# Forgetting attention in a two-layer trunk: one tile for a pair's transposed weights, and the values products at the pair's end

## The chip, the cores and the metric

The kernel runs on one core of one Trainium2 chip. The metric is the device time of one execution in microseconds (us). The kernel before was timed three times: median 1266.29 us, from 1264.41 to 1266.33. One more execution was profiled.

## What is computed

A decoder trunk of two layers on one sequence of 512 tokens with 1024 channels, in float32. Each layer mixes (two groups of heads, joined by an output projection), adds the residual, normalizes, and then runs a gated feed-forward. Only the mixer of layer 0 is touched here. Its two groups are HGRN2 (a gated linear recurrence, 4 heads of 128) and forgetting attention (8 heads of 64). The second one, cut to what matters:

```python
def forgetting_attention(q, k, v, f_logit, b_f):
    log_f = jax.nn.log_sigmoid(f_logit + b_f)
    c = jnp.cumsum(log_f, axis=1).transpose(0, 2, 1)
    for blk in range(S // Q_BLOCK):                 # 4 blocks of 128 queries
        q0, q1 = blk * Q_BLOCK, (blk + 1) * Q_BLOCK
        logits = einsum('bqhd,bkhd->bhqk', q[:, q0:q1], k[:, :q1]) * FOX_DIM ** -0.5
        logits = logits + c[:, :, q0:q1, None] - c[:, :, None, :q1]
        logits = where(kpos <= qpos, logits, -inf)
        p = softmax(logits, axis=-1)
        outs.append(einsum('bhqk,bkhd->bqhd', p, v[:, :q1]))
```

The last line is the values product of this text: query block i needs the i+1 key blocks up to its own, so a head has 1+2+3+4 = 10 blocks of 128 queries by 128 keys.

## The kernel before, in words

**Projections.** Every large product is done three times with operands split into a high and a low part (`mm3`, L245 to L249: high by high on L247, high by low on L248 or L249, and low by high on the other). A projection (`proj`) is 8 such triples of 512 columns into one PSUM bank, 24 products; `values` (L284) is four token blocks of 24 products. Weights come by DMA into `ws` (two buffers), ScalarE casts the high part `wh` (L236), VectorE makes the low part `wl` (L237); `wh` and `wl` have five buffers.

**Layer 0** (`layer0`) runs over four heads h. For each it writes down an HGRN2 head, then a pair of forgetting-attention heads; with h = 0 also the forget gates (`fox_gates`, L556 to L576) and the values of all pairs (`values(S_VB)`, names `pv` and then `v`), and with h = 3 the output projection (names `po` from `wh`, L326 for the residual). A scheduler reorders all of this for each engine ahead of the run, by dependences and by which buffers are free; the order on an engine is then fixed.

**An HGRN2 head.** `acc` (L476) takes the diagonal products `dg` (L475); then seven levels each make a tile `E` (VectorE L485, ScalarE exp L486, VectorE L487), small products `sc` (L493) and a masked copy into `acc` (L497). Beside these goes a state: `kd` (L504 to L506), its transposes `kt` (L510), the copy `kdt` (L512), products `st` (L516), the exp `eb` (L518) and the running state `stt` (L520, L523). Then `o` (L529, L531), its square `sq` on ScalarE (L534), the mean `ms` on TensorE (L536), ln and exp on ScalarE (L537, L538), two products on VectorE (L539, L540) and the split into `yh` and `yl` (L242, L243).

**The forget gates.** Products `pf` (L556), copied by ScalarE to the tile `f` (L559), folded by the product `pfb` (L563), whose result goes through ScalarE (L567 to L569) and VectorE (L570, L571, the scan L573), a cast to `c16h` (L575) and L576. The tiles `f` and `c16h` are drawn from the buffers named `pT`.

**A pair of attention heads** (`fox_pair`). The q and k projections are split per head into `qk` and `k` (VectorE L595, L600, L601; ScalarE L592, L594, L599). Then for each of four query blocks i: scores `s` (L627 to L629), row maximum (L632 or L638), exp and division on ScalarE (L640, L645; reciprocal L641), transposes of p into the PSUM tile `pt` (L647), one or two copies to the SBUF tile `pT` (L650, L652), the values products (L660; 2(i+1) of them, 128 columns wide, each with 64 rows of outputs), and at once the split of the block's 128 columns into `yh` (ScalarE L664) and `yl` (VectorE L665). For i = 0 and 1 both heads share one `pt`, one `pT` and one copy. `behind` keeps the first values product after the block's copies in the schedule.

**Buffers of layer 0** (2 KB per partition each): `E` 3, `pT` 2, and one each of `kd`, `kdt`, `eb`, `stt`, `sq`.

In layer 1 stick-breaking attention has the same shape of values products, already at a pair's end (L826).

Of the kernel before, what the change touches and what calls it, by code (L numbers as in the profile page):

```python
# [7 lines left out]
F32 = mybir.dt.float32  # L8
F32R = mybir.dt.float32r
# [3 lines left out]
ALU = mybir.AluOpType  # L13
AX = mybir.AxisListType

P = 128
T = 512
D = 1024
NTB = T // P
# [34 lines left out]
class Trunk:  # L54
# [373 lines left out]
    def hgrn_head(self, h, z=None, qp=None):  # L428
        nc = self.nc
# [4 lines left out]
        e = self.t2k("e", tag="E")  # L434
# [6 lines left out]
        bb = self.t2k("bb", [P, 2, T], tag="bb")  # L441
# [8 lines left out]
        kq = self.t2k("kq", [P, 2, T], tag="kq")  # L450
# [8 lines left out]
        G = self.t2k("G", tag="G")  # L459
# [8 lines left out]
        v = self.va  # L468

        hs = slice(h * P, (h + 1) * P)  # L470
        acc = self.t2k("acc", tag="acc")
# [6 lines left out]
        for li, w in enumerate(LEVELS):  # L478
            n = T // (2 * w)
            vw = lambda a: a.rearrange("p (n two w) -> p n two w", two=2, w=w)  # L480
            E = self.t2k("E", tag="E")
# [7 lines left out]
            for c in range(4):  # L489
                cc = slice(c * P, (c + 1) * P)  # L490
                rhs = E[:, cc].rearrange("p (n two w) -> p n two w", two=2, w=w)[:, :, 1, :]
                for u in (0, 64)[:1 if w == 64 else 2]:
                    nc.tensor.matmul(ps[u:u + 64, c * 64:(c + 1) * 64], E[:, c * P + u:c * P + u + 64], rhs,  # L493
                                     start=True, stop=True)
            m = slice(0, 64 if w == 64 else P)
# [2 lines left out]
                                      lv.rearrange("p c (n w) -> p c n w", w=w),  # L498
                                      ps[m, 0:256].rearrange("p (c n w) -> p c n w", c=4, w=w))

        kd = self.t2k("kd", tag="kd")
        b3 = b[:, 0:384].rearrange("p (c t) -> p c t", t=P)
        kd3 = kd[:, 0:384].rearrange("p (c t) -> p c t", t=P)
        nc.vector.tensor_tensor(kd3, b3[:, :, P - 1:P].to_broadcast([P, 3, P]), b3, ALU.subtract)  # L504
# [2 lines left out]
        pt = self.bank("ho", "kt")  # L507
        for c in range(3):
            cc = slice(c * P, (c + 1) * P)
            nc.tensor.transpose(pt[:, cc], kd[:, cc], self.ident)  # L510
        kdt = self.t2k("kdt", tag="kdt")
        nc.scalar.copy(kdt[:, 0:384], pt[:, 0:384])  # L512
        pst = self.bank("ho", "st")
        for c in range(3):
            cc = slice(c * P, (c + 1) * P)
            nc.tensor.matmul(pst[:, cc], kdt[:, cc], v[c][:, hs], start=True, stop=True)  # L516
        eb = self.t2k("eb", tag="eb")
        A(eb, b, AF.Exp)  # L518
        st = self.t2k("stt", tag="stt")
        nc.vector.tensor_copy(st[:, 0:P], pst[:, 0:P])  # L520
        for c in (1, 2):
            cc = slice(c * P, (c + 1) * P)
# [3 lines left out]
        po = self.bank("ho", "o")  # L526
# [3 lines left out]
            if c:  # L530
                nc.tensor.matmul(po[:, cc], st[:, (c - 1) * P:c * P], eb[:, cc], start=False, stop=True)  # L531

        sq = self.t2k("sq", tag="sq")
        A(sq, po, AF.Square)  # L534
        pm = self.bank("sc", "ms")
        nc.tensor.matmul(pm, self.cmean, sq, start=True, stop=True)  # L536
# [4 lines left out]
        yh, yl = self.act("yh"), self.act("yl")  # L541
# [4 lines left out]
    def fox_gates(self):  # L546
        nc = self.nc
        st = self.t2k("wfs", [P, NKB * 32], tag="p")
        nc.sync.dma_start(st, self.ins["wfb"])
        xs = self.xt.rearrange("p b (k t) -> p (b k) t", t=T)  # L550

        pf = self.bank("g", "pf4")
        for i in range(2):
            for g in range(4):
                kb = 4 * i + g
                nc.tensor.matmul(pf[32 * g:32 * g + 32, :], st[:, 32 * kb:32 * kb + 32], xs[:, kb, :], start=i == 0,  # L556
                                 stop=i == 1)
        f4 = self.t2k("f4", tag="pT")
        nc.scalar.copy(f4, pf)  # L559
        fold = self.odd.tile([P, 16], F32, name="fold")  # L560
        nc.vector.tensor_reduce(fold, self.ident.rearrange("p (g m) -> p m g", m=32)[:, 0:16, :], axis=AX.X, op=ALU.add)
        ps = self.bank("g", "pfb")
        nc.tensor.matmul(ps[0:16, :], fold, f4, start=True, stop=True)  # L563
        bf = self.par[0:16, C_BF:C_BF + 1]
        a = self.t2k("fa", tag="p")
        m = self.t2k("fm", tag="p")
        nc.scalar.activation(a[0:16], ps[0:16, :], AF.Abs, bias=bf)  # L567
        nc.scalar.activation(a[0:16], a[0:16], AF.Exp, scale=-1.0)
        nc.scalar.activation(a[0:16], a[0:16], AF.Ln, bias=self.one[0:16])  # L569
        nc.vector.tensor_scalar(m[0:16], ps[0:16, :], bf, 0.0, ALU.add, ALU.min)  # L570
        nc.vector.tensor_tensor(a[0:16], a[0:16], m[0:16], ALU.subtract)  # L571
        nc.gpsimd.memset(m[0:16], 1.0)
        nc.vector.tensor_tensor_scan(a[0:16], m[0:16], a[0:16], 0.0, ALU.mult, ALU.add)  # L573
        h16 = self.t2k("c16h", [16, T], F32R, tag="pT")
        nc.scalar.copy(h16, a[0:16])  # L575
        nc.vector.scalar_tensor_tensor(self.c16, h16.bitcast(F32), self.par[0:16, C_LOSEL:C_LOSEL + 1], a[0:16],  # L576
                                       ALU.mult, ALU.add)
# [26 lines left out]
    def fox_pair(self, hp, v):  # L604
        nc = self.nc
        A = nc.scalar.activation
        k2 = self.k2[hp % 2]
        for e in range(2):
            o, h = 64 - 64 * e, 2 * hp + e
            nc.gpsimd.dma_start(k2[e][o:o + 2].bitcast(F32), self.c16[2 * h:2 * h + 2].bitcast(F32))  # L610
        q, k = self.qk_pair(S_QB + hp, S_KB + hp, k2, self.q2)
        yh, yl = self.act("yh"), self.act("yl")
        po = self.bank("po", "po")
        for i in range(NTB):
            n = (i + 1) * P
            c = slice(i * P, n)

            both = 2 * n <= T
            ss = []
            for e in range(2):  # L620
                if e and both:
                    s = ss[0][0], n
                else:
                    s = self.bank("s", "s"), 0
                ss.append(s)
                ps = s[0][:, s[1]:s[1] + n]
                nc.tensor.matmul(ps, q[e][:, c], k[e][:, 0:n], start=True, stop=False)  # L627
                nc.tensor.matmul(ps, self.q2[e][:, c], k2[e][:, 0:n], start=False, stop=False)
                nc.tensor.matmul(ps[:, c], self.identb, self.foxmask, start=False, stop=True)  # L629
            nm, rs, ri = [self.small(x, [P, 2]) for x in ("nm", "rs", "ri")]  # L630
            if both:
                nc.vector.tensor_reduce(nm, ss[0][0][:, 0:2 * n].rearrange("p (e n) -> p e n", e=2), axis=AX.X,  # L632
                                        op=ALU.max, negate=True)
            ts, cps = [], []
            for e in range(2):
                ps = ss[e][0][:, ss[e][1]:ss[e][1] + n]
                if not both:
                    nc.vector.tensor_reduce(nm[:, e:e + 1], ps, axis=AX.X, op=ALU.max, negate=True)  # L638
                p = self.t2k("p", tag="p")
                A(p[:, 0:n], ps, AF.Exp, bias=nm[:, e:e + 1], accum_out=rs[:, e:e + 1])  # L640
                nc.vector.reciprocal(ri[:, e:e + 1], rs[:, e:e + 1])  # L641
                A(p[:, 0:n], p[:, 0:n], AF.Copy, scale=ri[:, e:e + 1])
                if not (both and e):
                    pt, pT = self.bank("pt", "pt"), self.t2k("pT", tag="pT")
                t0 = n if both and e else 0  # L645
                for j in range(i + 1):
                    nc.tensor.transpose(pt[:, t0 + j * P:t0 + (j + 1) * P], p[:, j * P:(j + 1) * P], self.ident)  # L647
                ts.append((pT, t0))
                if not both:
                    nc.vector.tensor_copy(pT[:, 0:n], pt[:, 0:n])  # L650
                elif e:
                    nc.vector.tensor_copy(pT[:, 0:2 * n], pt[:, 0:2 * n])  # L652
            cp = self.newest()

            for j in range(i + 1):
                for e in range(2):
                    h = 2 * hp + e
                    d = slice(64 * e, 64 * e + 64)
                    pT, t0 = ts[e]
                    nc.tensor.matmul(po[d, c], v[j][:, h * 64:h * 64 + 64], pT[:, t0 + j * P:t0 + (j + 1) * P],  # L660
                                     start=j == 0, stop=j == i)
                    if j == 0 and e == 0:
                        self.behind(self.newest(), cp)
            nc.scalar.copy(yh[:, c], po[:, c])  # L664
            nc.vector.tensor_tensor(yl[:, c], po[:, c], yh[:, c].bitcast(F32), ALU.subtract)  # L665
        return yh, yl

    def layer0(self):
# [183 lines left out]
@with_exitstack  # L852
def hybrid_trunk_kernel(ctx: ExitStack, tc: tile.TileContext, out, **ins):
    t = Trunk(tc, ctx, ins, out)
    t.setup()
    with t.phase("l0", v=8, p=2, pT=2, E=3, bb=1, kq=1, G=1, acc=1, kd=1, kdt=1, eb=1, stt=1, sq=1) as t.ph, \
            tc.tile_pool(name="odd", bufs=1) as t.odd:
        y = t.layer0()
    with t.phase("f0", s=3, wah=4, wal=4) as t.ph:
        wa = t.out_rows(y, S_WO0 + 4, 0, S_FFN0)  # L860
        wa = t.ffn(S_FFN0, wa, 1, S_XR)
        xr = t.proj_halves(wa)
    with t.phase("l1", v=4, qk=7, kz=2, z=6, l=4, sh=5, sl=5) as t.ph:
# [109 lines left out]
```

## Time and profile before

| | us |
|---|---|
| median of three runs | 1266.29 |
| the profiled execution | 1266.0 |
| its span on the core | 1264.2 |
| mean granted TensorE clock in it | 0.994 |

A line of a timeline or of the chain gives start, duration (us), engine, line and operation; "[1.05 <-DVE qk L600]" says that the engine stood idle 1.05 us before it and what it waited for. PE is TensorE (PEld its weight loads), DVE VectorE, ACT ScalarE. A number after x counts the instructions that are put together; an f32 product such as L660 counts as two instructions in the profile, so that the 20 values products of a pair are 40 there.

### The profile page before, as it was taken

The numbers are of one execution on the slowest core, as the hardware profiler recorded it, in microseconds if no ns is written. First come the engines' busy times: TensorE is split into PE (matmuls) and PEld (weight loads), VectorE is DVE, ScalarE is ACT, GpSimd is POOL, SyncE is SP. The second block draws the span as 40 slices with busy tenths as digits, with TensorE's granted clock in tenths as the row PEclk, the third lists the DMA queues.
The fourth block names the chain that finished last, engine by engine and source line by source line (L and its number), as shares of the span: only waits on it lengthen the run. The fifth ranks groups of instructions, "written<-read, shape, count | busy, mean of one in ns | idle before, by whom it ended". The sixth has DMA issues, their size and how long they took to land.

```text
span 1264.2 us, 15623 instructions
## 1 busy us (share of the span) xinstructions
PE 1244.6 (98%) x6311; PEld 1006.6 (80%) x6311; DVE 690.3 (55%) x1039; ACT 485.3 (38%) x748; POOL 28.9 (2%) x51
## 2 busy tenths in 40 slices
PE   9999999999999999999999999999999999999997
PEld 6787777779888888888889776777988888888885
DVE  7538788769334333334377596786733333433437
ACT  7446557442322222222233757673322222222120
POOL 2000000000000000000000000000000000000001
PEclk9999999999999999999999998999999999999999
DMA  6332111133232233332324221102423332333321
GB/s 237 117 112 63 61 51 51 51 117 103 98 99 90 96 99 100 100 94 91 99 91 143 67 86 48 48 20 84 151 67 100 100 98 87 99 101 100 100 67 67
DMA packets 34984, 115.46 MB, mean 91 GB/s; under 512 B 4176, under 2 KB 5200, under 8 KB 34912
## 3 DMA queue, kind: packets, MB, share of 16 engines
q1 hardware_dynamic: 33504, 112.77, 28.3%
q10 hardware_dynamic: 1152, 1.66, 0.4%
q8 instruction: 49, 0.80, 0.2%
q14 instruction: 23, 0.19, 0.0%
q0 software_dynamic: 256, 0.03, 0.0%
HBM read 112.32 MB, written 2.10 MB: 91 GB/s over the span
## 4 chain that ended last, share of the span: by engine, by line
PE 89%; DVE 6%; DMA 2%; ACT 2%; issue 1%; SPq 0%; DVEq 0%; ACTq 0%
PE pf L248 13%; PE pf L247 13%; PE pf L249 13%; PE po L249 8%; PE po L247 8%; PE po L248 8%; PE pj L247 5%; PE pj L248 5%; PE pj L249 4%; DMA ws<-in_wst 2%; PE sc L493 1%; PE po L660 1%; PE cu L815 1%; PE pv L248 1%; PE pv L247 1%; PE tr L317 1%
## 5 line engine op out<-in xcount | busy, mean ns | idle before, releaser
L236 ACT CAST wh<-ws 128x1024 fp32r<-128x1024 f32 x177 | 186.4, 1053 | 525.8 <-PE pf L248 190.5
L237 DVE TENSOR_TENSOR wl<-ws,wh 128x1024 fp32r<-128x1024 f32 x177 | 216.5, 1223 | 308.8 <-ACT wh L236 302.9
L247 PE MATMUL pf<-xh,wh 128*128 128x512 f32 x640 | 249.0, 389 | 0.0
L248 PE MATMUL pf<-xl,wh 128*128 128x512 f32 x640 | 249.0, 389 | 0.0
L249 PE MATMUL pf<-xh,wl 128*128 128x512 f32 x640 | 249.0, 389 | 0.0
L249 PEld LDWEIGHTS pf<-xh,wl 128*128 128x128 f32 x640 | 120.1, 188 | 25.1
L247 PEld LDWEIGHTS pf<-xh,wh 128*128 128x128 f32 x640 | 120.1, 188 | 24.9
L248 PEld LDWEIGHTS pf<-xl,wh 128*128 128x128 f32 x640 | 120.1, 188 | 24.7
L247 PE MATMUL po<-wh,hh 128*128 128x512 f32 x352 | 137.4, 390 | 0.0
L249 PE MATMUL po<-wh,hl 128*128 128x512 f32 x352 | 137.1, 390 | 0.1
L248 PE MATMUL po<-wl,hh 128*128 128x512 f32 x352 | 137.0, 389 | 0.0
L415 DVE TENSOR_TENSOR s<-s,pf 128x512 f32<-128x512 f32 x44 | 30.3, 688 | 141.8 <-PE pf L249 140.4
L247 PE MATMUL pj<-xh,wh 128*128 128x512 f32 x256 | 104.6, 410 | 1.7 <-DVE qk L595 1.1
L249 PE MATMUL pj<-xh,wl 128*128 128x512 f32 x256 | 105.4, 412 | 0.0
L248 PE MATMUL pj<-xl,wh 128*128 128x512 f32 x256 | 103.6, 405 | 0.0
L249 PEld LDWEIGHTS po<-wh,hl 128*128 128x128 f32 x352 | 66.0, 188 | 14.5 <-DVE hl L243 0.7
L247 PEld LDWEIGHTS po<-wh,hh 128*128 128x128 f32 x352 | 66.1, 188 | 14.3 <-DVE xt L328 0.6
L248 PEld LDWEIGHTS po<-wl,hh 128*128 128x128 f32 x352 | 66.1, 188 | 13.5
L247 PEld LDWEIGHTS pj<-xh,wh 128*128 128x128 f32 x256 | 48.4, 190 | 14.2 <-issue 4.6
L249 PEld LDWEIGHTS pj<-xh,wl 128*128 128x128 f32 x256 | 48.4, 189 | 10.6 <-issue 2.3
L248 PEld LDWEIGHTS pj<-xl,wh 128*128 128x128 f32 x256 | 48.4, 189 | 10.1 <-issue 1.4
L328 DVE TENSOR_TENSOR xt<-xt,po 128x512 f32<-128x512 f32 x64 | 43.4, 685 | 14.8 <-PE po L249 14.7
(242 smaller groups left out, 1818.7 us busy)
## 6 DMA issues: line engine op xcount, KB each, us to landing
ws<-in_wst SPq DMA_DIRECT2D x189, 512.0 KB, 3.5
gb<-in_lnp SPq DMA_DIRECT2D x8, 512.0 KB, 4.8
ws<-in_wst SPq DMA_DIRECT2D x12, 256.0 KB, 5.2
xt<-in_xT SPq DMA_DIRECT2D x8, 256.0 KB, 4.9
xt<-in_x SPq DMA_DIRECT2D x1, 2048.0 KB, 7.8
out_y<-xt SPq DMA_DIRECT2D x4, 256.0 KB, 2.0
out_y<-xt ACTq DMA_DIRECT2D x4, 256.0 KB, 2.0
gw<-in_gw ACTq DMA_DIRECT2D x2, 256.0 KB, 3.2
```

The lines of the kernel that those rows point to most:

```text
L236: nc.scalar.copy(hi, st)
L237: nc.vector.tensor_tensor(lo, st, hi.bitcast(F32), ALU.subtract)
L247: mm(ps, ah, bh, start=first, stop=False)
L248: mm(ps, ah, bl, start=False, stop=False)
L249: mm(ps, al, bh, start=False, stop=last)
L317: nc.tensor.transpose(ps[:, j * P:(j + 1) * P], y[:, h * T + j * P:h * T + (j + 1) * P], self.ident)
L328: self.nc.vector.tensor_tensor(y, y, ps, ALU.add)
L415: nc.vector.tensor_tensor(s, s, pb, ALU.mult)
L493: nc.tensor.matmul(ps[u:u + 64, c * 64:(c + 1) * 64], E[:, c * P + u:c * P + u + 64], rhs, start=True, stop=True)
L660: nc.tensor.matmul(po[d, c], v[j][:, h * 64:h * 64 + 64], pT[:, t0 + j * P:t0 + (j + 1) * P], start=j == 0, stop=j == i)
L815: nc.tensor.matmul(ps[:, c:c + m], w, x[:, oi:oi + m], start=n == 0 and x is sh, stop=n == len(mms) - 1 and x is sl)
```

## The change

The transposed weights of a pair are kept in one tile `pT` of 20 blocks of 128 columns (10 KB, one buffer). Each head's transposes get a copy of their own (now L657), which writes to every fifth or sixth block, so that all queries that use one key block lie side by side: for head 0 in blocks 15, 10 and so on downwards with the transposes in reversed order, for head 1 upwards. After the fourth query block come eight values products, for key blocks j = 0 to 3 and two heads, of 512, 384, 256 and 128 columns (L664). The result is split once, 512 columns wide, by `put` (L242, L243). For i = 0 and 1 there are two copies to SBUF instead of one.

To make room, `kd`, `kdt`, `eb`, `stt` and `sq` lose their own buffers and are drawn from `E`, which has five buffers instead of three; `f` and `c16h` of the forget gates, that were drawn from `pT`, are drawn from `E` too.

```diff
-        kd = self.t2k("kd", tag="kd")
+        kd = self.t2k("kd", tag="E")
...
-        sq = self.t2k("sq", tag="sq")
+        sq = self.t2k("sq", tag="E")
...
-        f4 = self.t2k("f4", tag="pT")
+        f4 = self.t2k("f4", tag="E")
...
-        h16 = self.t2k("c16h", [16, T], F32R, tag="pT")
+        h16 = self.t2k("c16h", [16, T], F32R, tag="E")
...
+        pT = self.t2k("pT", [P, 20 * P], tag="pT")
+        at = ((15, -6), (1, 5))
...
-                if not both:
-                    nc.vector.tensor_copy(pT[:, 0:n], pt[:, 0:n])
-                elif e:
-                    nc.vector.tensor_copy(pT[:, 0:2 * n], pt[:, 0:2 * n])
+                    m = j if step > 0 else i - j
+                    nc.tensor.transpose(pt[:, t0 + m * P:t0 + (m + 1) * P], p[:, j * P:(j + 1) * P], self.ident)
+                lo = o + i + (0 if step > 0 else i * step)
+                dst = bass.AP(tensor=pT.tensor, offset=pT.offset + lo * P,
+                              ap=[pT.ap[0], [abs(step) * P, i + 1], [1, P]])
+                nc.vector.tensor_copy(dst, pt[:, t0:t0 + n].rearrange("p (j t) -> p j t", t=P))
+        cp = self.newest()
+
+        for j in range(NTB):
+            for e in range(2):
+                h = 2 * hp + e
+                x = (at[e][0] + at[e][1] * j + j) * P
+                nc.tensor.matmul(po[64 * e:64 * e + 64, j * P:T], v[j][:, h * 64:h * 64 + 64], pT[:, x:x + T - j * P],
+                                 start=j == 0, stop=j == NTB - 1)
...
-            nc.scalar.copy(yh[:, c], po[:, c])
-            nc.vector.tensor_tensor(yl[:, c], po[:, c], yh[:, c].bitcast(F32), ALU.subtract)
+        self.put(po, yh, yl)
...
-    with t.phase("l0", v=8, p=2, pT=2, E=3, bb=1, kq=1, G=1, acc=1, kd=1, kdt=1, eb=1, stt=1, sq=1) as t.ph, \
+    with t.phase("l0", v=8, p=2, pT=1, E=5, bb=1, kq=1, G=1, acc=1) as t.ph, \
```

The change moves more than its own lines. TensorE's order in head 0, before: `sc` are the level products, `pfb` the folding of the gates, `pv` the first token block of the values projection.

```order
L493 MATMUL sc_514<-E_510 64x64 x8
L563 MATMUL pfb_622<-f_80_618,fold 16x512
L247 MATMUL pv_664<-wh_642,xh 128x512
L493 MATMUL sc_528<-E_524 64x64 x8
L248 MATMUL pv_664<-wl_643,xh 128x512
L249 MATMUL pv_664<-wh_642,xl 128x512
L247 MATMUL pv_664<-wh_642,xh 128x512
L248 MATMUL pv_664<-wl_643,xh 128x512
L249 MATMUL pv_664<-wh_642,xl 128x512
L493 MATMUL sc_542<-E_538 64x64 x8
```

The same place of the changed kernel (`kt` and `st` belong to the state, `o` and `ms` to the head's end):

```order
L493 MATMUL sc_528<-E_524 64x64 x8
L510 MATMUL kt_570<-ident,kd_566 128x128 x3
L516 MATMUL st_576<-v_305,kdt_574 128x128
L516 MATMUL st_576<-v_306,kdt_574 128x128
L516 MATMUL st_576<-v_307,kdt_574 128x128
L493 MATMUL sc_542<-E_538 64x64 x8
L493 MATMUL sc_556<-E_552 64x64 x8
L529 MATMUL o_587<-acc_465,v_305 128x128
...
L536 MATMUL ms_597<-sq_595,cmean 128x512
L563 MATMUL pfb_622<-f_80_618,fold 16x512
L247 MATMUL pv_664<-wh_642,xh 128x512
```

The folding and the whole first values block now stand behind the last level and behind `ms`, and the state's transposes and products stand between the levels. On ScalarE the copy of `f`, which the folding needs, has moved behind the square; before:

```order
L486 ACTIVATE E_524<-E_524 128x512
L559 COPY f_80_618<-pf_79_609 128x512
L486 ACTIVATE E_538<-E_538 128x512
L567 ACTIVATE fa_624<-pfb_622,par 16x512
L486 ACTIVATE E_552<-E_552 128x512
```

And in the changed kernel, where the copy takes a buffer of `E`, which are drawn in the order of the program, after `sq`:

```order
L518 ACTIVATE eb_580<-bb_252 128x512
L534 ACTIVATE sq_595<-o_587 128x512
L559 COPY f_80_618<-pf_79_609 128x512
L537 ACTIVATE sq_595<-ms_597,eps 128x512
L538 ACTIVATE sq_595<-sq_595 128x512
```

VectorE's order at the entry of the last pair (h = 3), before: `sq` and `yl` end the HGRN2 head, `wl` is a weight, `qk` and `k` are the two heads' keys, for which the scores wait.

```order
L539 TENSOR_TENSOR sq_2209<-sq_2209,o_2201 128x512
L540 TENSOR_TENSOR sq_2209<-sq_2209,G_2073 128x512
L237 TENSOR_TENSOR wl_2591<-ws_2588,wh_2590 128x1024
L243 TENSOR_TENSOR yl_2218<-sq_2209,yh_2217 128x512
L600 CAST qk_2223<-pj_2267 64x512
L601 TENSOR_TENSOR k_233<-pj_2267,qk_2223 64x512
L326 SCALAR_TENSOR_TENSOR xt<-xt,po_2459 128x512
L600 CAST qk_2223<-pj_2267 64x512
```

In the changed kernel:

```order
L539 TENSOR_TENSOR sq_2146<-sq_2146,o_2138 128x512
L600 CAST qk_2160<-pj_2204 64x512
L540 TENSOR_TENSOR sq_2146<-sq_2146,G_2010 128x512
L601 TENSOR_TENSOR k_233<-pj_2204,qk_2160 64x512
L237 TENSOR_TENSOR wl_2507<-ws_2504,wh_2506 128x1024
L243 TENSOR_TENSOR yl_2155<-sq_2146,yh_2154 128x512
L600 CAST qk_2160<-pj_2204 64x512
```

The first head's key moved ahead of the weight, the second head's stands behind the weight and `yl`. On TensorE, 9 instead of 12 products of the output projection lie ahead of this pair's first scores, 3 between them and the second part of those scores, and none between the first head's scores and the second's (4 before).

More of the change, by code (lines that the diff above doesn't have):

```diff
@@ L510, in hgrn_head @@
             nc.tensor.transpose(pt[:, cc], kd[:, cc], self.ident)
-        kdt = self.t2k("kdt", tag="kdt")
+        kdt = self.t2k("kdt", tag="E")
         nc.scalar.copy(kdt[:, 0:384], pt[:, 0:384])
@@ L516, in hgrn_head @@
             nc.tensor.matmul(pst[:, cc], kdt[:, cc], v[c][:, hs], start=True, stop=True)
-        eb = self.t2k("eb", tag="eb")
+        eb = self.t2k("eb", tag="E")
         A(eb, b, AF.Exp)
-        st = self.t2k("stt", tag="stt")
+        st = self.t2k("stt", tag="E")
         nc.vector.tensor_copy(st[:, 0:P], pst[:, 0:P])
@@ L633, in fox_pair @@
                                         op=ALU.max, negate=True)
-            ts, cps = [], []
             for e in range(2):
@@ L643, in fox_pair @@
                 if not (both and e):
-                    pt, pT = self.bank("pt", "pt"), self.t2k("pT", tag="pT")
+                    pt = self.bank("pt", "pt")
                 t0 = n if both and e else 0
+                o, step = at[e]
                 for j in range(i + 1):
-                    nc.tensor.transpose(pt[:, t0 + j * P:t0 + (j + 1) * P], p[:, j * P:(j + 1) * P], self.ident)
-                ts.append((pT, t0))
-                if not both:
-                    nc.vector.tensor_copy(pT[:, 0:n], pt[:, 0:n])
-                elif e:
-                    nc.vector.tensor_copy(pT[:, 0:2 * n], pt[:, 0:2 * n])
[L653 to L665, printed above, removed]
+                    m = j if step > 0 else i - j
[11 more added lines that the diff above has]
+                                 start=j == 0, stop=j == NTB - 1)
+                if j == 0 and e == 0:
+                    self.behind(self.newest(), cp)
+        self.put(po, yh, yl)
         return yh, yl
```

## The prediction

> **What bounds the kernel now.** I read the page first, then the busy time by stage, then the chain, then timelines at the places that the change touches. The page gives the span and TensorE's share, and the chain of work that ended last gives its parts by engine.
>
> ```profile
> span 1264.2 us, 15623 instructions
> PE 1244.6 (98%) x6311; PEld 1006.6 (80%) x6311; DVE 690.3 (55%) x1039; ACT 485.3 (38%) x748; POOL 28.9 (2%) x51
> PE 89%; DVE 6%; DMA 2%; ACT 2%; issue 1%; SPq 0%; DVEq 0%; ACTq 0%
> ```
>
> TensorE is the bound: 98% busy and 89% of the chain. So two things count, TensorE's own work and the moments at which it has nothing to do. Layer 0 by stages shows the few of these; the columns are stretch, length, busy time of PE, PEld, DVE, ACT and POOL with their instructions, then the granted clock. The first stretch is the levels of head 0 to the end of the first values block, the next ones are the rest up to the end of pair 0, 1, 2 and 3.
>
> ```profile
> 46.15:66.00 19.85, 19.65 (x182) 12.75 (x180) 15.44 (x27) 9.60 (x16) 1.72 (x3) 1.00 0.48 173
> 66.00:121.00 55.00, 55.00 (x279) 42.49 (x278) 31.65 (x55) 30.41 (x60) 2.12 (x5) 1.00 0.27 81
> 169.70:218.50 48.80, 48.80 (x343) 36.32 (x343) 38.88 (x75) 29.72 (x62) 0.00 (x0) 1.00 0.14 45
> 218.50:266.00 47.50, 46.25 (x324) 33.87 (x323) 34.36 (x64) 24.47 (x51) 0.00 (x0) 0.96 0.22 74
> ```
>
> TensorE has no idle time in pairs 0 and 2 and 1.25 us in pair 3. What is taken from its work there shortens the run one for one, and a new gap lengthens it one for one.
>
> **Term 1, the values products: a gain of 6.3.** The chain shows all values groups of pair 2 (start, us, instructions), and the last row is layer 1's L826, which has the new form: 512, 384, 256 and 128 columns for two heads, in one group.
>
> ```profile
> 202.39 0.37 PE po L660 x4
> 206.25 0.59 PE po L660 x8
> 209.44 0.36 PE po L660 x2
> 210.47 0.80 PE po L660 x10
> 214.88 0.36 PE po L660 x2
> 215.90 1.02 PE po L660 x14
> 805.47 2.83 PE po L826 x14
> ```
>
> The six groups are 40 instructions and 0.37 + 0.59 + 0.36 + 0.80 + 0.36 + 1.02 = 3.50 us; the twin takes 2.83. Around a group something is lost as well, as TensorE's timeline shows in pair 0:
>
> ```profile
> 110.41 0.50 PE L248 MATMUL pj<-xl,wh 128*128 128x512 f32 x1
> 110.74 0.40 PE L249 MATMUL pj<-xh,wl 128*128 128x512 f32 x1
> 111.07 0.87 PE L660 MATMUL po<-pT,v 128*64 128x128 f32 x10
> 111.87 0.50 PE L247 MATMUL pj<-xh,wh 128*128 128x512 f32 x1
> 112.20 0.40 PE L248 MATMUL pj<-xl,wh 128*128 128x512 f32 x1
> 65.93 0.23 PE pv L249
> ```
>
> Projection products of 512 columns follow each other every 0.23 us (the last row, of the chain), but from 110.74 to the group's start are 0.33, and from the group's end (111.87) to the second product after it 0.33 again: 0.10 on entry and 0.10 on exit. Of the six groups five lie between projection products and are charged 0.20; the group of eight lies between score products, where I charge half. Before: 3.50 + 5 x 0.20 + 0.10 = 4.60. After: 2.83 + 0.20 = 3.03. The gain is 1.57 a pair, 6.3 for four. It is bounded by 4 x 0.67 = 2.7 (no entry or exit is real) and 4 x 1.67 = 6.7 (all six charged). I take 6.3, since the 0.33 stand right at such a group.
>
> The Trainium skill, page "TensorE: Matmul & The Clock Gate", section "Back-to-back issue gap", gives N/2.4 + about 2.5 ns from one product to the next; by an estimate from that, 40 instructions of 128 columns and 16 of 512 to 128 cost 2.23 and 2.17 us a pair, so that this term would be 0.2 and not 6.3. The rows speak against it: 1.02 us for 14 instructions of 128 columns is 73 ns each, not 56.
>
> **Term 2, head 0: a loss of 5.4.** Between the levels of head 0 TensorE waits for VectorE. Before, the folding `pfb` and the first values block filled these gaps. In the changed kernel both stand behind the last level, `o` and `ms`, since `f` needs a buffer of `E` and its copy stands behind the square on ScalarE. VectorE's waits between the levels, then the head's end in the chain and on the two other engines:
>
> ```profile
> 49.38 0.44 DVE L497 COPY_PREDICATED acc<-lvl,sc 64x256 f32<-64x256 uint8 x1 [1.22 <-PE sc L493]
> 50.87 0.46 DVE L497 COPY_PREDICATED acc<-lvl,sc 128x256 f32<-128x256 uint8 x1 [0.28 <-PE sc L493]
> 52.38 0.69 DVE L487 TENSOR_TENSOR E<-E,kq 128x512 f32<-128x512 f32 x1 [0.48 <-ACT E L486]
> 60.48 0.73 DVE L497 COPY_PREDICATED acc<-lvl,sc 128x256 f32<-128x256 uint8 x1 [0.75 <-PE sc L493]
> 61.39 0.61 PE L529 MATMUL o<-acc,v 128*128 128x128 f32 x4
> 62.87 0.48 PE L248 MATMUL pv<-wl,xh 128*128 128x512 f32 x1
> 63.27 0.58 ACT L534 ACTIVATE sq<-o 128x512 f32<-128x512 f32 x1
> 64.38 0.86 PE ms L536 x2
> 54.25 0.96 PE pfb L563 x2
> ```
>
> The last level's copy ends at 60.48 + 0.73 = 61.2. I leave it there: two weight casts (`wl`), the state's `kd` and `eb` come in among VectorE's level work, and four passes over `E`, `fm` and `fa` go out, about 3.8 us each way. Then, with nothing between: `o` from 61.4 to 62.9, the square from 63.27 to 63.85, `ms` 0.86 to about 64.9 with its start, `pfb` 0.96 to 65.9, and 24 products of 0.23, at 5.5 us, to 71.4. Before, this block was done at 66.0: plus 5.4. From there TensorE is busy for 55.00 of 55.00 us, so nothing takes the loss back. Lower bound: without any of the four waits (1.22 + 0.28 + 0.48 + 0.75 = 2.7) the copy ends at 58.5, and the loss is 2.7. Upper: the state's chain (exp, transposes, copy, products), that now stands between the levels, lies wholly on the path, at about 2.5 by its parts before: 7.9. I take the middle one, since both effects work on the same copies.
>
> **Term 3, the clock: a loss of 1.7.** In pair 3 TensorE stood idle once for over a microsecond, and the clock fell; the columns are those of the stages.
>
> ```profile
> 245.00:246.00 1.00, 1.00 (x4) 0.75 (x4) 0.97 (x2) 0.00 (x0) 0.00 (x0) 0.61 0.04 16
> 246.00:247.00 1.00, 1.00 (x5) 0.91 (x4) 0.17 (x1) 0.00 (x0) 0.00 (x0) 0.50 0.00 0
> 247.00:248.00 1.00, 1.00 (x6) 0.70 (x6) 0.40 (x1) 0.00 (x0) 0.00 (x0) 0.50 0.00 0
> 248.00:249.00 1.00, 1.00 (x5) 0.82 (x5) 0.47 (x3) 0.94 (x5) 0.00 (x0) 0.68 0.00 0
> 243.54 0.47 PE L627 MATMUL s<-qk 128*128 128x128 f32 x2 [1.05 <-DVE qk L600]
> ```
>
> The clock is lost for 0.39 + 0.50 + 0.50 + 0.32 = 1.7 of 4 us. Head 0 of the changed kernel has gaps of that size between its levels, one after another, and I charge one such fall there, 1.7, with bounds of none and of two and a half (4.0). The Trainium skill's same page, section "HAM oscillation — how this bites in real kernels", says "no PE-idle gaps >~3.4µs"; by that rule gaps of this size would cost no clock, and the sum below would be +1.6. This case's trace differs: a wait of 1.05 us was followed by the fall.
>
> **Term 4, the entries of the pairs: a loss of 1.5.** At a pair's entry TensorE's scores wait for the keys that VectorE splits. These rows are VectorE's in pair 3:
>
> ```profile
> 239.54 0.69 DVE L539 TENSOR_TENSOR sq<-sq,o 128x512 f32<-128x512 f32 x1 [3.57 <-PE pj L248]
> 240.88 1.22 DVE L237 TENSOR_TENSOR wl<-ws,wh 128x1024 fp32r<-128x1024 f32 x1
> 242.71 0.68 DVE L600 CAST qk<-pj 64x512 fp32r<-64x512 f32 x1
> ```
>
> In the changed kernel's order and with these durations, VectorE does `sq` at 239.54, the first L600 till 240.95, L540, the first L601 till 242.2, the weight till 243.3, `yl` till 244.0, the second L600 till 244.8 and L601 till 245.4. TensorE goes through the rest of the projection and 9 products till 241.1, the first scores till 241.5, 3 products and the second part of the scores till 242.8, and then waits for the second L600: 2.0, and 0.3 more for L601. That is 2.3 in place of 1.25, plus 1.0 (bounds: no wait at all, minus 1.3, and every split late by a weight's 1.22, plus 2.3). In pair 1 the same count ends within half a microsecond of a wait: 0.5 (0 to 2.5). In pair 2 none.
>
> **Term 5, the transposes: a loss of 1.0.** For i = 0 and 1 the second head's transposes write to the PSUM bank from which the first head's copy is now read, and wait for it. The nearest row is the 128-column split, the first one here:
>
> ```profile
> L665 DVE TENSOR_TENSOR yl<-po,yh 128x128 fp32r<-128x128 f32 x16 | 4.6, 287 | 2.4 <-ACT yh L664 2.2
> L664 ACT CAST yh<-po 128x128 fp32r<-128x128 f32 x16 | 4.2, 263 | 6.2 <-PE po L660 6.1
> ```
>
> Eight such copies of 0.29 are 2.3 if TensorE waits out each, and 0 if the projection's products cover them; with the copy itself queued on VectorE I take 1.0 (0 to 2.5).
>
> **Nothing** comes from the splits. Per pair ScalarE loses 4 x 0.263 and VectorE 4 x 0.287 and each gets one of 512 columns back; they are 38% and 55% busy, and after the pair's end the output projection is far off, except in pair 3, where later products cover it; uncovered it would cost one split, 0.6.
>
> **Sum:** -6.3 + 5.4 + 1.7 + 1.5 + 1.0 = +3.3. The profiled execution took 1266.0 (span 1264.2 and 1.8 around it), so 1269.3; it lies 0.3 under the median of the runs shown, so I say 1269.6 on their scale.
>
> **The rivals.** 0.2%, or 2.5 us, is about what a measurement of this kernel tells from no change.
>
> *A. Faster: VectorE doesn't wait.* Without the fillers TensorE serves each level at once, VectorE runs through head 0 without its 2.7 us of waits, and the state's chain hides beside it. With the clock whole and the entries free this gives -6.3 + 2.7 = -3.6: 1262.7. It decides once the last L497 of head 0 ends before about 59.6 and none of the other terms is there. For it: three of the four waits are for TensorE. Against: the state's chain now stands between the levels, and 3.8 us of new VectorE work. Chance 0.27.
>
> *B. No change to be measured.* Head 0 costs its 5.4, but gaps, entries and transposes together no more than 1.0: -6.3 + 5.4 + 1.0 = +0.1, so 1266.4. For it: most waits before were covered by projection products. Chance 0.24.
>
> *C. The half clock comes back.* A fall in pairs 1 and 3 and a second one in head 0 add 3 x 1.7 = 5.1: +8.4, 1274.7. The trace shows that one wait of 1.05 us is enough. Chance 0.10.
>
> *D. Products cost by their columns.* If a narrow product costs only its columns and entry and exit are hidden, 40 instructions at 73 ns are 2.92 against 2.83, and term 1 is 4 x 0.09 = 0.4 only: +9.2, 1275.5. Against it stand the 0.33. The Trainium skill's rule for the gap between products, weighed above, is of this kind. Chance 0.06.
>
> **How the numbers follow.** The forecast (slower by 0.26%, from 1268.8 to about 1272) has 0.33, so slower has 0.33 + 0.10 + 0.06 = 0.49, same 0.24, faster 0.27. The range goes from 1262.0, which holds most of A (its far end, 1261.4, has the entry of pair 3 free as well), to 1276.0, which holds C and D.
>
> **What would show it.** In head 0 of the changed profile: level products with idle time in front of them and no `pv` between, the last L497 at about 61, `pfb` after `ms`, the first `pv` block done at about 71, a granted clock below 1.00 near it. Values groups of L664 of about 2.83 with 0.33 at each end. An idle time of some 2 us before the second L631 in pair 3. The forecast is wrong if the first `pv` block is done by 69, if the clock stays whole through head 0, or if the values groups of a pair take over 4 us.

## The result, and the profile after

| | us |
|---|---|
| kernel before, median of 4 runs | 1266.19 (1264.41 to 1266.33) |
| changed kernel, median of 4 runs | 1274.65 (1272.92 to 1276.18) |
| ratio, 95% interval | 1.0069 (1.0053 to 1.0085) |
| profiled execution of the changed kernel | 1272.92, span 1270.8, mean granted clock 0.990 |

Slower, and by more than forecast: 8.5 us on the medians where 3.3 were said. The profiled execution is the fastest of the four; the other three took 1274.2 to 1276.2 us at a granted clock of 0.987. Of the changed kernel the page's span, busy times and chain by engine:

```profile
span 1270.8 us, 15388 instructions
PE 1243.4 (98%) x6215; PEld 1006.7 (79%) x6215; DVE 691.7 (54%) x1035; ACT 484.0 (38%) x736; POOL 28.8 (2%) x51
PE 87%; DVE 6%; ACT 3%; DMA 2%; issue 1%; SPq 0%; DVEq 0%; ACTq 0%
```

TensorE has 96 instructions and 1.2 us less to do, and the span is 6.6 us longer. So look for idle time. TensorE's timeline in head 0, its first products (`dg`) and then from the fourth level to the end of the first values block (some rows between are left out):

```profile
47.02 1.05 PE L475 MATMUL dg<-kq 128*128 128x128 f32 x8
54.79 0.69 PE L493 MATMUL sc<-E 128*64 128x64 f32 x16 [1.86 <-DVE acc L497]
56.70 0.69 PE L493 MATMUL sc<-E 128*64 128x64 f32 x16 [1.23 <-DVE acc L497]
62.24 1.12 PE L493 MATMUL sc<-E 128*64 128x64 f32 x16 [0.82 <-DVE acc L497]
64.19 1.22 PE L529 MATMUL o<-acc,v 128*128 128x128 f32 x4 [0.82 <-DVE acc L497]
68.30 1.12 PE L536 MATMUL ms<-sq,cmean 128*128 128x512 f32 x2 [0.75 <-ACT sq L534]
69.35 1.03 PE L563 MATMUL pfb<-f,fold 128*16 128x512 f32 x2
70.31 0.50 PE L247 MATMUL pv<-wh,xh 128*128 128x512 f32 x1
75.66 0.39 PE L249 MATMUL pv<-wh,xl 128*128 128x512 f32 x1
75.89 0.39 PE L247 MATMUL pv<-wh,xh 128*128 128x512 f32 x1
```

The levels now wait for VectorE's copies with no folding and no values product in between (the state's transposes and products stand between the fifth and the sixth), then come `o`, `ms`, `pfb`, and the first block's 24 products run from 70.31 to 75.89; before, they were done at 66.00. The level at 62.24 has 16 instructions like those at 54.79 and 56.70, but takes 1.12 us instead of 0.69: the clock. The folding is so late because ScalarE copies `f` only behind the square (before, at 53.53):

```profile
68.14 0.58 ACT L559 COPY f<-pf 128x512 f32<-128x512 f32 x1
```

The head also began a little later. In the profile of the kernel before, its first products stand here:

```profile
46.38 1.05 PE L475 MATMUL dg<-kq 128*128 128x128 f32 x8
```

The same stretch of the changed kernel by windows (before the last three columns, the granted clock):

```profile
46.38:57.00 10.62, 7.53 (x94) 4.30 (x94) 7.34 (x13) 4.25 (x6) 0.00 (x0) 1.00 0.67 213
57.00:68.00 11.00, 8.28 (x69) 6.91 (x65) 4.34 (x9) 1.36 (x3) 0.00 (x0) 0.53 0.44 178
68.00:75.89 7.89, 7.59 (x29) 5.02 (x29) 4.48 (x6) 5.05 (x9) 0.52 (x1) 1.00 0.01 2
```

For 11 us the clock was 0.53, though TensorE was busy for 8.28 of them; in the four us ahead of the fall (53 to 57) it had been busy for 0.98 only. The values groups of the four pairs, in the chain:

```profile
125.14 2.45 PE po L664 x15
172.29 2.76 PE po L664 x13
218.33 2.90 PE po L664 x14
267.06 2.92 PE po L664 x14
```

The entry of pair 3 in the changed kernel's timeline,

```profile
251.43 0.50 PE L631 MATMUL s<-qk 128*128 128x128 f32 x2 [1.82 <-DVE qk L600]
252.16 0.48 PE L632 MATMUL s<-k,q 128*128 128x128 f32 x1 [0.23 <-DVE k L601]
```

and the clock right after it, by windows:

```profile
252.00:256.00 4.00, 3.84 (x12) 3.15 (x13) 2.02 (x6) 1.50 (x6) 0.00 (x0) 0.57 0.25 102
```

That is 4 x 0.43 = 1.7 us of clock lost, as much as the fall in pair 3 of the kernel before. The end of layer 0, where the first transposes of the normalized rows start, before:

```profile
285.32 1.33 PE L317 MATMUL tr<-ident,xt 128*128 128x128 f32 x8
```

and in the changed kernel:

```profile
291.16 1.33 PE L317 MATMUL tr<-ident,xt 128*128 128x128 f32 x8
```

So at the end of head 0 TensorE is late by 75.89 - 66.00 = 9.9, and 0.6 of this lay ahead of the head (47.02 - 46.38); at the end of layer 0 it is late by 5.8: the rest of the layer gave 4.1 back. The remaining 0.8 of the span arise behind it, in work that the change doesn't touch.

### The profile page after: what moved, and what is told of

The parts are those of the page before. It is cut to its first block, busy times and chain, and to the rows that moved or that the text cites. A ratio compares the mean times of both kernels' runs of the same rounds, so it can differ in the third digit from the quotient of the medians.

```text
span 1270.8 us, 15388 instructions
## 1 busy us (share of the span) xinstructions
PE 1243.4 (98%) x6215; PEld 1006.7 (79%) x6215; DVE 691.7 (54%) x1035; ACT 484.0 (38%) x736; POOL 28.8 (2%) x51
## 4 chain that ended last, share of the span: by engine, by line
PE 87%; DVE 6%; ACT 3%; DMA 2%; issue 1%; SPq 0%; DVEq 0%; ACTq 0%
PE pf L248 13%; PE pf L247 12%; PE pf L249 12%; PE po L249 8%; PE po L247 8%; PE po L248 8%; PE pj L247 4%; PE pj L248 4%; PE pj L249 4%; DMA ws<-in_wst 2%; PE sc L493 1%; PE cu L818 1%; PE pv L247 1%; PE pv L249 1%; PE pv L248 1%; PE tr L317 1%
## 5 line engine op out<-in xcount | busy, mean ns | idle before, releaser
L247 PE MATMUL po<-wh,yh 128*128 128x512 f32 x128 | 51.4, 402 | 0.0
```

What stands on the lines that cost most here:

```text
L247: mm(ps, ah, bh, start=first, stop=False)
```

## The experiments

My theory was that the place of `f` in `E` costs head 0 its fillers, and that the attention gains. Rivals: the state's tiles in `E` cost (S), or the new attention loses by its entries (N). Three kernels tell these apart, and one more is on the width of the products.

**f out of E.** The changed kernel with the gates' two tiles taken from the `pT` tile, which is free then:

```diff
-        f4 = self.t2k("f4", tag="E")
+        f4 = self.t2k("f4", [P, 20 * P], tag="pT")[:, 0:T]
...
-        h16 = self.t2k("c16h", [16, T], F32R, tag="E")
+        h16 = self.t2k("c16h", [P, 20 * P], tag="pT").bitcast(F32R)[0:16, 0:T]
```

> The changed kernel, but with the two tiles of the forget gates (f, c16h) drawn from the pT tile instead of from E; everything else as changed. My theory (the place of f costs head 0 its fillers): the first values block of head 0 is done at 66 to 67 us again instead of 75.9, no half clock there, and the total falls from 1274.65 by 8 to 12 us, to 1262 to 1266. Rival S (the state's tiles drawn from E, which put its transposes and products between the levels, are what costs): head 0 stays over 5 us late, total 1270 to 1274.

Measured: 1262.79, ratio to before 0.9981 (0.9972 to 0.9989). From TensorE's timeline the last product of the first values block, the first of the next, and pair 3's entry:

```profile
64.84 0.39 PE L249 MATMUL pv<-wh,xl 128*128 128x512 f32 x1
65.07 0.40 PE L247 MATMUL pv<-wh,xh 128*128 128x512 f32 x1
241.61 0.50 PE L631 MATMUL s<-qk 128*128 128x128 f32 x2 [1.81 <-DVE qk L600]
```

By windows, all of head 0 and the ten us around that entry:

```profile
46.42:66.60 20.18, 19.86 (x183) 13.00 (x182) 13.75 (x24) 9.57 (x16) 2.80 (x5) 1.00 0.57 206
240.00:250.00 10.00, 8.17 (x35) 6.09 (x35) 6.98 (x18) 4.37 (x15) 0.00 (x0) 0.83 0.16 53
```

The block is done at 65.1, the clock is whole, TensorE busy for 19.86 of 20.18 us. (`ms`, which stood ahead of the block's end before, stands behind it here; at the third product of the next block the two kernels are level, 66.42 against 66.45, so head 0 is as quick as before and not quicker.) Two lines of the change turned a gain into a loss. The stall in pair 3 is still there, with the fall of the clock (0.83 over ten us).

**The buffers alone.** The kernel before, with all seven tiles drawn from `E` and its phase line changed:

```diff
-    with t.phase("l0", v=8, p=2, pT=2, E=3, bb=1, kq=1, G=1, acc=1, kd=1, kdt=1, eb=1, stt=1, sq=1) as t.ph, \
+    with t.phase("l0", v=8, p=2, pT=2, E=5, bb=1, kq=1, G=1, acc=1) as t.ph, \
```

> The kernel before with the old attention, but with all the buffers of the change: kd, kdt, eb, stt, sq and f, c16h drawn from E with five buffers. My theory (the buffers cost about 10 in head 0, the attention gains about 4 to 6): 1275 to 1280, slower than the changed kernel. Rival N (the buffers cost less, and the new attention itself loses through its entries and copies): 1268 to 1272, faster than the changed kernel.

Measured: 1276.35, ratio 1.0091 (1.0077 to 1.0104). Its head 0 waits like the changed kernel's (timeline),

```profile
63.42 1.23 PE L529 MATMUL o<-acc,v 128*128 128x128 f32 x4 [0.82 <-DVE acc L497]
67.53 2.07 PE L536 MATMUL ms<-sq,cmean 128*128 128x512 f32 x2 [0.75 <-ACT sq L534]
```

and its clock falls for at least as long (it is still 0.50 from 68 to 70):

```profile
57.00:68.00 11.00, 7.99 (x56) 6.86 (x55) 3.81 (x8) 2.08 (x4) 0.00 (x0) 0.52 0.40 163
```

N falls: with the old attention the buffers alone cost about as much as the whole change or more (1.0091 against 1.0069; the intervals touch).

**The state in E alone.** As the one above, but `f` and `c16h` left on the `pT` buffers.

> The kernel before with the old attention, with only the state's tiles and the square (kd, kdt, eb, stt, sq) drawn from E with five buffers; f and c16h stay where they were. My theory: 1265 to 1268, since the fillers stay between the levels. Rival S (the state's place between the levels costs by itself): 1270 to 1274.

Measured: 1265.10, ratio 0.9998 (0.9989 to 1.0007). S falls too: the state's products stand between the last levels here as well,

```profile
57.80 0.94 PE L516 MATMUL st<-v,kdt 128*128 128x128 f32 x6
```

and cost nothing that can be measured as long as the fillers stand there. (Pair 3 of this kernel also ran without the long stall of the kernel before, with a wait of 0.55 us and a whole clock; the control further down prices that at about 0.1%, so a cost of that size could hide here.) Between this kernel and the last one only the place of two tiles differs: 11.2 us.

**Narrow products at the end.** The first kernel (f out of E), with the products in one group at the pair's end but 128 columns wide:

```diff
-        for j in range(NTB):
-            for e in range(2):
...
+        for i in range(NTB):
+            for j in range(i + 1):
+                for e in range(2):
...
+                    nc.tensor.matmul(po[64 * e:64 * e + 64, i * P:i * P + P], v[j][:, h * 64:h * 64 + 64],
+                                     pT[:, x:x + P], start=j == 0, stop=j == i)
```

> The first kernel of this call (f out of E), with the values products at the pair's end in one group, but 20 of 128 columns instead of 8 of 512 to 128. Theory G (what is saved is the group's start, entry and exit): a group takes about 2.9 us beside 2.83, and the total is within 1.0 of the first kernel's. Rival W (what is saved is the width): a group takes 3.5 or more, and the total is 3 to 6 above the first kernel's.

Measured: 1257.24, ratio 0.9938 (0.9925 to 0.9952), and neither theory had it: 5.5 below the first kernel. The groups of the first and the last pair in the chain,

```profile
115.18 2.33 PE po L665 x40
253.91 2.33 PE po L665 x40
```

and, from the timeline, the only wait for keys in pair 3:

```profile
239.48 0.33 PE L632 MATMUL s<-k,q 128*128 128x128 f32 x1 [0.83 <-DVE k L601]
```

40 narrow instructions take 2.33 us, less than 16 wide ones (2.45 to 2.92). The same 40 instructions took 3.50 us in six groups before, so one group instead of six saves 1.17 a pair, and width adds nothing to that. Against the wide groups of the first kernel, four narrow ones explain 4 x 2.33 = 9.3 against 2.45 + 2.76 + 2.88 + 2.92 = 11.0, or 1.7 of the 5.5. The scheduler had also come to another order in pair 3: the stall of 1.8 us, and the fall of the clock behind it, are gone. The next kernel tests whether that is the rest.

**Keys first.** The first kernel, with one line that holds the third weight of the output projection behind the pair's last key on VectorE:

```diff
-            nc.vector.tensor_tensor(lo, st,     hi.bitcast(F32), ALU.subtract)
+            nc.vector.tensor_tensor(lo, st,     hi.bitcast(F32), ALU.subtract); idx == S_WO0 + 2 and self.behind(self.newest(), self.klast)
...
-        return qs, ks
+        self.klast = self.newest(); return qs, ks
```

> The kernel with f out of E (wide products at the pair's end), with one weight's low part (the third of the output projection's weights) held behind the last key of its pair on VectorE, so that the keys of pair 3 come first. Theory P (that weight ahead of the second key costs an idle time of about 2 us and a fall of the clock): the wait before the second L631 of pair 3 falls from 1.8 to under 0.5, the clock stays 1.00 there, and the total falls from 1262.79 to 1258.5 to 1260.5. Rival: another wait takes its place, and the total stays within 1261.5 to 1264.

Measured: 1258.72, ratio 0.9943 (0.9929 to 0.9956), some 4 below the kernel without that line, as theory P said. What is left of the stall,

```profile
240.20 0.33 PE L632 MATMUL s<-k,q 128*128 128x128 f32 x1 [0.23 <-DVE k L601]
```

and the clock of those ten us:

```profile
240.00:250.00 10.00, 9.80 (x50) 7.33 (x51) 9.43 (x22) 6.96 (x19) 0.00 (x0) 1.00 0.40 115
```

**Heads apart, and halves.** Two kernels, run once each, for what a group's time consists of; in the first one the two loops over j and e are exchanged.

> The kernel with f out of E, with the same eight wide products at a pair's end, but head 0's four first and then head 1's four, instead of alternating. Theory Q (the two heads write to different halves of the output rows and run beside each other in the array): a group takes 4.2 to 5.0 us instead of 2.83. Rival (products run one after another and cost by their columns): still 2.8 to 3.0.

> The kernel with f out of E, with 12 products of 256 and 128 columns at the pair's end instead of 8 of 512 to 128, the heads alternating. Theory Q (the second head starts one instruction of the first head's later, so a wide first product costs its own length): a group takes 2.5 to 2.6 us, between 2.40 (128 columns) and 2.83 (512). Rival (a product has a fixed start): 2.9 or more.

Totals 1267.64 and 1258.57. The groups of pair 0 with heads apart:

```profile
115.67 2.30 PE po L664 x8
118.06 1.46 PE po L664 x6
```

and with halves, pair 0 and pair 2, with the next head's `dg` between, eight instructions of 128 columns that fill all 128 output rows:

```profile
115.35 2.31 PE po L667 x24
119.25 0.89 PE dg L475 x8
207.46 2.46 PE po L667 x23
```

Apart, 3.8 us; alternating, 2.3 to 2.9. Theory Q holds in kind: a head's products fill 64 of the 128 output rows, and two heads run beside each other if they alternate. Two sizes say so: eight instructions, as many as one head has, take 2.30 us apart, and both heads together take 2.31 alternating; and `dg` takes 0.11 us for an instruction of 128 columns, where the 40 narrow ones take 2.33 / 40 = 0.058. Theory Q's size was off: apart was expected at 4.2 or more, and since 3.8 is less than twice 2.30, the second head must start before the first is through; no row shows where. The Trainium skill, page "TensorE: Matmul & The Clock Gate", section "Part 3: Packing small matmuls — row/col tiling", says that several matmuls may run concurrently in one array if each addresses its own tile; the 3.8 against 2.3 agree with that. That a wide first product delays the second head by one instruction was too simple: with 256 columns three pairs of four show no more delay than with 128 (2.31, once 2.46), with 512 it was anything from 0.1 to 0.6. Why it varies stays open. The kernel with halves also shows a wait in pair 3, of the length that the kernel before has there, but with no fall of the clock in its stretch:

```profile
238.56 0.47 PE L631 MATMUL s<-qk 128*128 128x128 f32 x2 [1.09 <-DVE qk L600]
236.00:246.00 10.00, 8.76 (x44) 6.31 (x42) 8.18 (x17) 4.16 (x15) 0.00 (x0) 1.00 0.16 54
```

**The clock held.** The changed kernel itself, `f` in `E`, with unread products behind four levels of head 0:

```diff
-            m = slice(0, 64 if w == 64 else P)
+            h == 0 and li >= 3 and self.hold(); m = slice(0, 64 if w == 64 else P)
...
+    def hold(self):
+        last = self.newest()
+        pd = self.bank("po", "dm")
+        for _ in range(4):
+            self.nc.tensor.matmul(pd, self.xh[:, 0, 0:P], self.xh[:, 0, :], start=True, stop=True)
+            self.behind(self.newest(), last)
```

> The changed kernel (f in E), with four products of 512 columns, whose result nobody reads, behind each of head 0's last four levels, about 0.9 us in each gap, to keep TensorE busy. Theory C (about 3 to 4 of head 0's loss are the half clock, the rest is waiting): the clock stays 1.00 in head 0, its first values block is done at 72 to 73.5 instead of 75.9, the total falls from 1274.65 to 1270 to 1272.5. Rival (VectorE sets the pace there, so that the clock costs nothing, or the clock falls anyhow): 1274 to 1277.

Measured: 1271.48, ratio 1.0046 (1.0032 to 1.0059). The clock in head 0,

```profile
50.00:68.00 18.00, 14.46 (x146) 9.39 (x146) 9.88 (x18) 5.54 (x10) 0.00 (x0) 1.00 0.46 177
```

and the fourth level, `o` and the product behind the first values block in the timeline:

```profile
53.72 0.69 PE L493 MATMUL sc<-E 128*64 128x64 f32 x16 [1.46 <-DVE acc L497]
63.19 0.71 PE L529 MATMUL o<-acc,v 128*128 128x128 f32 x4 [1.22 <-DVE stt L523]
73.56 0.39 PE L247 MATMUL pv<-wh,xh 128*128 128x512 f32 x1
```

The clock stays whole, though TensorE still waits 1.46 and 1.22 us at a time, and the block is done at 73.6 instead of 75.9. But `o` now waits for the state, whose products stood behind the last unread ones; the cure took part of its own gain. A further kernel puts the unread products behind the third to fifth level only (`li in (2, 3, 4)`):

> As the changed kernel with unread products that keep TensorE busy in head 0, but behind the third, fourth and fifth level only, so that the state's products stand ahead of the last level again as in the changed kernel, and no unread product stands ahead of them. Theory C2 (the waiting alone costs what was forecast, 5.4, and the rest of head 0's loss is the half clock, 4 to 4.5): clock whole, first values block done at 71 to 72.3, total 1269 to 1271. Rival (the half clock was worth only the 2.3 seen before, and the levels wait longer than forecast): block done at 73 or later, total 1271 to 1272.5.

Measured: 1268.54, ratio 1.0020 (1.0010 to 1.0029). The clock in head 0,

```profile
57.00:68.00 11.00, 9.29 (x79) 6.28 (x75) 4.97 (x10) 4.22 (x8) 0.00 (x0) 1.00 0.42 170
```

and the head's first products and the product behind the first values block:

```profile
46.59 1.05 PE L475 MATMUL dg<-kq 128*128 128x128 f32 x8
72.23 0.39 PE L247 MATMUL pv<-wh,xh 128*128 128x512 f32 x1
```

With the clock whole the block is done at 72.2. From the head's first products to there it takes 25.6 us, where the kernel before takes 19.6 and the changed kernel 28.9: the waiting costs 6.0, the half clock 3.2, and the other 0.6 of the 9.9 lie ahead of the head. (If the unread products hold anything up themselves, the waiting costs less and the half clock more.) On the medians twelve products that nobody reads win back 0.49% (1.0069 against 1.0020) of the whole time, some 6 us, give or take 2.4 by the two intervals. The total came a little below what C2 said.

**Everything together.** Two versions with f out of E and keys first, and the kernel before with keys first as a control.

> f out of E, products of 256 and 128 columns at the pair's end, and the third output weight held behind pair 3's keys. If what was found holds (a group of halves takes 2.3 to 2.4 us where the wide ones took 2.45 to 2.92, and no stall of about 2 us with a fall of the clock in pair 3): 1256 to 1258, some 1.5 below the wide kernel with the keys first (1258.72). Rival: another wait opens in pair 3, and it is 1258.5 to 1262.

> f out of E, 20 products of 128 columns at the pair's end, and the third output weight held behind pair 3's keys. Its sister without that hold had no stall of 2 us already and took 1257.24, with one wait of 0.8 for a key. If the hold only takes that wait away: 1256 to 1257.3. Rival (the moved weight comes late for the output projection): 1257.5 or more.

> The kernel before, unchanged but for the third output weight held behind pair 3's keys. It tells how much of the gain of the kernels with keys first has nothing to do with the attention's products. If the wait of 1.05 us in pair 3 and the fall of the clock behind it go: 1262.5 to 1264.3 where the kernel before takes 1265 to 1266. Rival (a wait of over 1 us remains and the clock falls all the same): 1265 to 1266.5.

Measured: halves 1258.63, ratio 0.9938 (0.9926 to 0.9951); narrow 1257.69, 0.9933 (0.9920 to 0.9945); the control 1264.72, 0.9991 (0.9982 to 1.0000), with this rest of its stall:

```profile
243.88 0.50 PE L627 MATMUL s<-qk 128*128 128x128 f32 x2 [0.18 <-DVE qk L600]
```

and this clock around it:

```profile
240.00:250.00 10.00, 9.59 (x50) 6.61 (x48) 8.82 (x17) 4.84 (x15) 0.00 (x0) 1.00 0.15 54
```

The halves missed their range by 0.6: their groups are 0.4 us a pair shorter than the wide ones, but the total is that of the wide kernel with keys first. The narrow products gain nothing from the moved weight (1257.24 and 0.9938 without it). Both totals so lie on the side of their rivals, though no new wait of a microsecond is there; at this distance the kernels can't be told apart. The four timed versions with `f` out of `E` and no long stall in pair 3 lie between 0.9933 and 0.9943 with overlapping intervals, some 7 to 8 us faster than before. The control lies between its two theories: the stall and the fall of the clock are gone, and that alone is worth about 0.1% (0.2% at most by the interval).

## Why the prediction was right or wrong, point by point

**Direction and place: right.** Head 0 went as written: levels waiting with no `pv` between, `pfb` behind `ms`. The experiments show the cause, two tiles that `E` hands out in program order. The times were later than the signs said: the last copy of a level ended at 64.1 (61 said) and the block at 75.9 (71 said).

**Term 1, the values products, forecast 6.3: right in sum, half wrong in reason.** Without the stall, new against old attention is 0.9943 against 0.9991, 0.48% or 6.1 us, give or take 2.0. The profiles of these two kernels agree: layer 0 ends 6.2 us earlier (0.3 of it lie ahead of head 0), at

```profile
277.12 1.33 PE L317 MATMUL tr<-ident,xt 128*128 128x128 f32 x8
```

with the new attention, and in the control at

```profile
283.33 1.34 PE L317 MATMUL tr<-ident,xt 128*128 128x128 f32 x8
```

In the changed kernel's own profile the gain is the 4.1 behind head 0 and the 0.8 of the longer stall, 4.9. In the groups themselves 14.0 (4 x 3.50) became 11.0 us; the other half I had put to their entries and exits, which no run took by themselves. But part of it I put to width, and the narrow kernel has as much. I read 1.02 us for 14 as 73 ns each; the quoted rows held better: 10 took 0.80 and 14 took 1.02, so four more cost 0.22, 55 ns each, and a group has a fixed part of 0.15 to 0.25 us; five of a pair's six fixed parts went. The Trainium skill's 56 ns (same page, "Back-to-back issue gap"), which I weighed and set aside, has the size of that, and of 40 in 2.33 us (58 ns). But this is no agreement in kind: one such instruction on all 128 rows takes 111 ns (`dg`), and only two heads beside each other bring it to 58. The estimate from the Trainium skill was right that width brings nothing, and did not speak of groups.

**Term 2, the waits of head 0, forecast 5.4: 6.0** with the clock held. The last copy ended at 61.7 there (61.2 forecast).

**Term 3, the clock, forecast 1.7: the mis-sized term.** I charged one fall such as the one in pair 3. In the profile it lasted from 57 to 68 us and cost 3.2, within the bounds (0 to 4.0); the medians (1.0069 against 1.0020) give about 6, beyond them. The other three executions had a lower clock (0.987 against 0.990), which fits a longer fall, but no trace shows it. Rival C, which has the clock fall more often, came nearest to the time (1274.7 against 1274.65), but by luck: the fall in pair 1 did not come, the one in pair 3 was there before and cost no more than before, and the one in head 0 was twice to four times as dear as the 1.7 that C charges a fall. The Trainium skill's "no PE-idle gaps >~3.4µs" (same page, "HAM oscillation — how this bites in real kernels") would have allowed these gaps; none was over 1.86 us, and the clock halved. Nor does my own rule hold, that a wait of about a microsecond is enough: the kernel with halves waited 1.09 us in pair 3 and the first kernel with unread products 1.46 us in head 0, both with the clock whole.

**Term 4, the entries, forecast 1.5:** pair 3 waited 1.82 + 0.23 instead of 1.05 + 0.16, plus 0.8 (1.0 said); in pair 1 no wait (0.5 said). The wait came where and how the text said, before the second head's L631.

**Term 5, the transposes, forecast 1.0: nothing.** No transposes wait for a copy of the weights in the profile; their only wait, 0.25 us in pair 0, is put down to ScalarE's `bb` (L448).

**The rest:** all that was forecast behind head 0 is -6.3 + 1.5 + 1.0 = -3.8; it was 5.8 - 9.9 = -4.1. In the profile the span grew by 6.6 where 3.3 were said: 1.5 more for the clock, 0.6 more for the waits, 1.4 outside what the change touches (0.6 ahead of head 0, 0.8 behind layer 0), and 0.3 less for the rest. On the medians the miss is 5, and most of it is the clock, about 6 (give or take 2.4) where 1.7 were charged.

## What to carry to other kernels

When tiles are moved to a shared pool, look at the order of allocation: an early, small tile that now queues behind a late one can take its readers, and everything behind them, out of the gaps that they filled. Where TensorE loses its fillers for some ten us, count its clock as well as the waiting, over the whole stretch and not for one fall. Useless products in the gaps can be cheaper than the gaps. Before a group is widened, take the price of an instruction from the difference of two rows, not from a quotient that holds the group's start, and look at what else runs beside it.

## What the runs showed of the hardware that was not expected

The clock was half for about 10 us while TensorE was busy for three quarters of the time, behind four us with 0.98 us of work and gaps of 1.86 us and less; unread products of 0.9 us behind three levels kept it whole. The length of one gap did not decide: it fell behind 1.05, 1.81 and 1.82 us in pair 3, and not behind 1.09 there or 1.46 and 1.22 in head 0. What does decide is not shown. Two heads' products of 64 output rows each run beside each other when they alternate (2.3 us, 40 narrow or 24 half-wide instructions) and for a small part only when they don't (3.8 us); 16 wide ones take 2.4 to 2.9 for the same columns.
